# Two heads of attention share the products with their inverse sums; the norm of x is spread over the context's FFN, and that FFN's last products move to its end

## The chip, the cores and the metric

The kernel runs on one core of a Trainium2 chip. The metric is device time in microseconds (us), the median of several runs. One further execution is recorded by the hardware profiler; the profile gives its own time and its span, from its first instruction to its last.

## The reference, cut to what matters

Two layers work on a stream x of 512 tokens and a context of 256 tokens, both 1024 wide and in float32. A layer normalises its input, projects it, mixes it (attention, a Fourier mixer, a long convolution), projects the mix back and adds it; then it normalises again and applies a gated feed-forward network (FFN) with a convolution over three neighbouring tokens. The context is updated in the first layer only.

```python
s = einsum('bqhgd,bkhd->bhgqk', q, k) * (HEAD_DIM ** -0.5)   # 8 heads of 64, 2 kv heads
p = softmax(s, axis=-1)                                      # x sees 768 keys, the context 256
attn = einsum('bhgqk,bkhd->bqhgd', p, v)
...
u = dwconv3(h @ w_up, w_c, b_c)                              # 1024 -> 2 * 2816
gate, val = split(u, 2)
y = (silu(gate) * val) @ w_down                              # 2816 -> 1024
...
ctx = ctx + cga2 * rmsnorm(yc, g_post_ffn[i])                # first layer only
hc  = rmsnorm(ctx, g_pre_mix[1]) * (1.0 + csc1) + csh1       # what the second layer reads of it
```

## The kernel before, in words

**Products.** TensorE multiplies in a short float format, so each float32 factor is split into a high and a low part (`split`: a cast on ScalarE, L179, and a subtraction on VectorE or GpSimd, L180), and three products (`mm3`, L194 to L196) make one. Weights are loaded by SyncE's DMA queue into two buffers `Wr` (or `L`, `Wm`), and split into `Wh` and `Wl`.

**Order.** The kernel is written with Python generators. `go` runs a main piece and lets fillers run between its steps; `add` queues a filler in a lane; `need` runs a filler to its end. A table `Z` of waits and shares decides when each may go on. The tile framework then places the instructions of each engine in a fixed order; an engine takes its instructions in that order only.

**Attention** (`scores`, `attention`, `attention_small`, `head_out`). For a head and a tile of 128 queries, TensorE makes the scores, VectorE their maximum (L1010), ScalarE the exponentials `p` and their sum `den` (L1014). TensorE turns `p` (L1059), the halves of the turned tile `pT` are made, and TensorE multiplies them with the values (L1046) into `acc`, which holds the head's output as channels by queries, 64 rows from the high values and 64 from the low ones. To divide by the sums, TensorE multiplies the inverse sums, broadcast along 128 columns, with the identity (L1051 for x, four products a head; L1120 for the context, two a head): every row of the result `rb` holds the inverse sum of each query. `head_out` adds the two halves of `acc` (L1130, L1131) and multiplies them with `rb` (L1132), on 64 of the 128 partitions, because two heads share one tile `mix`. The scores run about one head ahead of the products with the values.

**First layer, second half.** `mix_out` of x leaves four tiles of x and queues, for each, the norm that the FFN of x reads (`norm_tile7`: four products with a diagonal matrix `dg`, L361, and four scalings on VectorE, L435, for each half tile; for tiles 2 and 3 also sums of tiles, L446 to L451, and splits `h<-xr` on VectorE and GpSimd). These norms, named `norm_xf0` to `norm_xf3`, are fillers of the context's FFN (`ffn_c`). That FFN makes 22 blocks m of 128 channels (`up`: 48 products, then the convolution L655 to L657, silu, the gate multiply on GpSimd L1301, and the split into `gc`), and after each second block the down products of the two blocks before (`ffn_down`, added to `y` at L1249). The last two blocks' down products are kept as a generator `rest_c`. Then `norm_xf3` must be done, and the FFN of x (`ffn_x`) runs: 22 blocks m, each with seven half-size products of sums of tiles and of weights. The sums of weights, `tt`, are made by GpSimd (L1348 to L1351, `prep`), then split (`Wh<-tt`, `Wl<-tt`). The entry `'RC': 3` puts `rest_c` behind block 3 of `ffn_x`. `rest_c` ends with the residual of the context (`rstd`, L221 to L227; L1155), and queues `tail_c`: the norm of the context for the second layer (`norm_tile`, with the scalings on VectorE, L404, or on ScalarE, L406, as its argument `dve` says; `NC` holds that argument), whose result is stored to memory.

Of the kernel before, what the change touches and what calls it, by code (L numbers as in the profile page):

```python
# [11 lines left out]
AF = mybir.ActivationFunctionType  # L12
ALU = mybir.AluOpType
# [4 lines left out]
P = 128  # L18
# [33 lines left out]
C512, C256, CTR, CF512 = 0.216, 0.109, 0.109, 0.86  # L52
# [13 lines left out]
class Net:  # L66
# [930 lines left out]
    def scores(self, st, h, t):  # L997
        nc = self.nc
        NK = 768 if st is self.X else 256
        kv = h // (NH // NKV)  # L1000
        hp = 1024 // st.T
        Q = st.Q[h // hp][:, h % hp]
        segs = [(0, 512), (512, 768)] if NK == 768 else [(0, 256)]
        ps = self.pw()
        qs = slice(t * P, (t + 1) * P)
        for a, b in segs:
            nc.tensor.matmul(ps[:, a:b], Q[:, qs], self.KD_[kv][:, a:b], start=True, stop=False)
            nc.tensor.matmul(ps[:, a:b], Q[:, qs], self.KL_[kv][:, a:b], start=False, stop=True)
        nm = self.small("nmax", 1, 4)
        nc.vector.tensor_reduce(nm, ps[:, :NK], axis=AX.X, op=ALU.max, negate=True)  # L1010
        p = self.M("p", F32)[:, :NK]
        if t == 0:
            st.den[h] = self.small("den", 4, 3)
        nc.scalar.activation(p, ps[:, :NK], AF.Exp, bias=nm, scale=1.0, accum_out=st.den[h][:, t : t + 1])  # L1014
        st.p[h, t] = p
        if t == st.NT - 1:
            nc.vector.reciprocal(st.den[h][:, : st.NT], st.den[h][:, : st.NT])
        return 2 * C512 * NK / 512

    def attention(self, st):  # L1020
        nc = self.nc
        NKT = 6 if st is self.X else 2
        T, NT = st.T, st.NT
        st.p, st.den = {}, {}
        todo = [(h, t) for h in range(NH) for t in range(NT)]
        lead = NT + Z["lead"]

        def ahead(n):
            c = 0.0
            for _ in range(n):  # L1030
                if todo:
                    c += self.scores(st, *todo.pop(0))
            return c

        yield ahead(2), Z["at0"]
        yield ahead(lead - 2), Z["at1"]
        LAG = 2
        acc, pts = {}, {}

        def pv(h, kt):  # L1040
            if kt == 0:
                acc[h] = self.pn()[:, :T]
            v = self.V_[h // (NH // NKV)][:, kt]
            pT = pts.pop((h, kt))
            for e in range(2):
                nc.tensor.matmul(acc[h], v, pT[:, e], start=kt == 0 and e == 0, stop=kt == NKT - 1 and e == 1)  # L1046
            if kt < NKT - 1:
                return 2 * C512 * T / 512
            rb = self.pn()[:, :T]
            for t in range(NT):  # L1050
                nc.tensor.matmul(rb[:, t * P : (t + 1) * P], st.den[h][:, t : t + 1].broadcast_to([P, P]), self.ident, start=True, stop=True)  # L1051
            self.head_out(st, h, acc[h], rb)
            return NT * 0.22 + 2 * C512 * T / 512

        steps = [(h, kt) for h in range(NH) for kt in range(NKT)]
        for i, (h, kt) in enumerate(steps):
            pt = self.pn()
            for t in range(NT):
                nc.tensor.transpose(pt[:, t * P : (t + 1) * P], st.p[h, t][:, kt * P : (kt + 1) * P], self.ident)  # L1059
            pT = self.M("pT").rearrange("p (e t) -> p e t", e=2)[:, :, :T]  # L1060
            self.split(pT[:, 0], pT[:, 1], pt[:, :T])
            pts[h, kt] = pT
            c = NT * CTR
            if NKT == 6:
                c += ahead(1 if kt < NT else 0)
            else:
                c += ahead(1)
            if i >= LAG:
                c += pv(*steps[i - LAG])
            yield c, 0.0  # L1070
        for i in range(LAG):
            yield pv(*steps[len(steps) - LAG + i]), 0.0

    def attention_small(self, st):

        nc = self.nc
        T, NT = st.T, st.NT
# [3 lines left out]
        for i in range(NH + 2):  # L1081
            c = 0.0
            if i < NH:
                kv = i // g
                Q = st.Q[i // hp][:, i % hp]
                ps = self.pn()
                sc = ps.rearrange("p (t k) -> p t k", t=NT)
                for t in range(NT):
                    qs = slice(t * P, (t + 1) * P)
                    nc.tensor.matmul(sc[:, t], Q[:, qs], self.KD_[kv][:, 0:T], start=True, stop=False)  # L1090
                    nc.tensor.matmul(sc[:, t], Q[:, qs], self.KL_[kv][:, 0:T], start=False, stop=True)
                nm = self.small("nmax2", NT, 4)
                nc.vector.tensor_reduce(nm, sc, axis=AX.X, op=ALU.max, negate=True)
                p = self.M("p", F32)[:, : NT * T].rearrange("p (t k) -> p t k", t=NT)
                den = self.small("den", 4, 3)
                for t in range(NT):
                    nc.scalar.activation(p[:, t], sc[:, t], AF.Exp, bias=nm[:, t : t + 1], scale=1.0, accum_out=den[:, t : t + 1])
                nc.vector.reciprocal(den[:, :NT], den[:, :NT])
                ps_[i], dens[i] = p, den
                c += 4 * C256  # L1100
            if 0 <= i - 1 < NH:
                p = ps_.pop(i - 1)
# [7 lines left out]
                c += 4 * CTR  # L1110
            if i >= 2:
                h = i - 2
                pT, den = pTs.pop(h), dens.pop(h)
                ps = self.pn()
                acc, rb = ps[:, 0:T], ps[:, T : 2 * T]
                for kt in range(NT):
                    for e in range(2):
                        nc.tensor.matmul(acc, self.V_[h // g][:, kt], pT[:, e, kt * T : (kt + 1) * T], start=kt == 0 and e == 0, stop=kt == NT - 1 and e == 1)
                for t in range(NT):
                    nc.tensor.matmul(rb[:, t * P : (t + 1) * P], den[:, t : t + 1].broadcast_to([P, P]), self.ident, start=True, stop=True)  # L1120
                self.head_out(st, h, acc, rb)
                c += 4 * C256 + NT * 0.22
            yield c, Z["as"]

    def head_out(self, st, h, acc, rb):
        nc = self.nc
        b0 = 64 * (h % 2)
        me, ot = slice(b0, b0 + 64), slice(64 - b0, 128 - b0)
        tf, of = self.T(st.T, "tf"), self.T(st.T, "of")
        nc.scalar.copy(tf[me], acc[ot])  # L1130
        nc.vector.tensor_tensor(of[me], acc[me], tf[me], op=ALU.add)  # L1131
        nc.vector.tensor_tensor(self.mixf(st, h // 2)[me], of[me], rb[me], op=ALU.mult)  # L1132
# [147 lines left out]
    def ffn_c(self, l):  # L1280
# [183 lines left out]
    def run(self):  # L1464
# [27 lines left out]
        for l in range(2):  # L1492
# [284 lines left out]
```

## Time and profile before

| what | value |
|---|---|
| median of 3 runs | 1768.56 us (1767.65 to 1769.28) |
| the profiled execution: its time | 1770.96 us |
| the profiled execution: its span | 1769.2 us |
| TensorE (PE) busy with products | 1640.4 us, 93% |
| VectorE (DVE) | 1391.0 us, 79% |
| ScalarE (ACT) | 949.8 us, 54% |
| GpSimd (POOL) | 672.2 us, 38% |
| mean granted clock of TensorE | 0.969 |

Every table of the profile is of the one profiled execution. A busy share over the whole span mixes stages; a stage is read with the windows view, which gives the busy time of each engine between two times and the granted clock (PEclk, 1.00 is full speed). The waits view says who waited for whom. A group row reads: line, engine, operation, output<-inputs, shapes, count | busy us, mean ns of one | idle us of the engine just before them.

### The profile page before, as it was taken

The numbers are of one execution on the slowest core, as the hardware profiler recorded it, in microseconds if no ns is written. First come the engines' busy times: TensorE is split into PE (matmuls) and PEld (weight loads), VectorE is DVE, ScalarE is ACT, GpSimd is POOL, SyncE is SP. The second block draws the span as 40 slices with busy tenths as digits, with TensorE's granted clock in tenths as the row PEclk, the third lists the DMA queues.
The fourth block names the chain that finished last, engine by engine and source line by source line (L and its number), as shares of the span: only waits on it lengthen the run. The fifth ranks groups of instructions, "written<-read, shape, count | busy, mean of one in ns | idle before, by whom it ended". The sixth has DMA issues, their size and how long they took to land. (4 is left out here: it accounts for less than half of the span.)

```text
span 1769.2 us, 27894 instructions
## 1 busy us (share of the span) xinstructions
PE 1640.4 (93%) x10534; PEld 1400.9 (79%) x10534; DVE 1391.0 (79%) x2269; ACT 949.8 (54%) x1787; POOL 672.2 (38%) x495
## 2 busy tenths in 40 slices
PE   6899988899999998998899998998899799999997
PEld 2677765787788897887889985787787678999995
DVE  3776667697666698888899997668895978989996
ACT  3554354586565454555555555534874455555553
POOL 2342212000134348664465545312002456555543
PEclk9899998999999998999999998999999799999999
DMA  9224377603476642233243358654012343323323
GB/s 361 92 77 140 88 226 267 231 11 143 164 254 229 227 153 82 86 108 96 72 138 113 96 168 320 214 176 132 1 48 82 128 137 119 105 88 106 96 74 129
DMA packets 75314, 246.69 MB, mean 139 GB/s; under 512 B 8111, under 2 KB 9647, under 8 KB 75180
## 3 DMA queue, kind: packets, MB, share of 16 engines
q1 hardware_dynamic: 66348, 215.54, 36.4%
q0 software_dynamic: 8832, 29.37, 5.4%
q8 instruction: 83, 1.36, 0.3%
q14 instruction: 51, 0.42, 0.1%
HBM read 230.72 MB, written 14.16 MB: 138 GB/s over the span
## 5 line engine op out<-in xcount | busy, mean ns | idle before, releaser
L194 PE MATMUL pn<-h,Wh 128*128 128x256 f32 x1328 | 374.4, 284 | 10.9 <-DVE C L1398 3.4
L196 PE MATMUL pn<-h,Wl 128*128 128x256 f32 x1328 | 370.2, 282 | 7.6 <-DVE Wl L180 7.6
L195 PE MATMUL pn<-h,Wh 128*128 128x256 f32 x1328 | 371.9, 281 | 1.9 <-POOL h L180 1.9
L194 PEld LDWEIGHTS pn<-h,Wh 128*128 128x128 f32 x1328 | 251.8, 190 | 21.2 <-issue 4.4
L196 PEld LDWEIGHTS pn<-h,Wl 128*128 128x128 f32 x1328 | 251.3, 190 | 11.7 <-DVE Wl L180 9.0
L195 PEld LDWEIGHTS pn<-h,Wh 128*128 128x128 f32 x1328 | 252.7, 190 | 5.9 <-POOL h L180 2.1
L179 ACT CAST Wh<-Wr 128x1024 fp32r<-128x1024 f32 x118 | 123.5, 1050 | 137.3 <-PE pn L195 63.1
L1348 POOL TENSOR_TENSOR tt<-r,r 128x512 f32<-128x512 f32 x44 | 66.0, 1501 | 260.7 <-DMA r<-w_up 224.8
L180 DVE TENSOR_TENSOR Wl<-Wr,Wh 128x1024 fp32r<-128x1024 f32 x89 | 121.5, 1367 | 53.2 <-ACT Wh L179 52.7
L195 PE MATMUL pw<-Wl,gT 128*128 128x512 f32 x352 | 141.0, 401 | 2.0 <-DVE Wl L180 2.0
L194 PE MATMUL pw<-Wh,gT 128*128 128x512 f32 x352 | 136.3, 403 | 5.3 <-ACT Wh L179 2.6
L196 PE MATMUL pw<-Wh,gT 128*128 128x512 f32 x352 | 139.7, 398 | 0.0
L180 DVE TENSOR_TENSOR Wl<-tt,Wh 128x1024 fp32r<-128x1024 f32 x88 | 129.8, 1495 | 7.5 <-ACT Wh L179 7.5
L1407 POOL TENSOR_TENSOR ft<-ft,ft 128x512 f32<-128x512 f32 x44 | 66.6, 1513 | 145.0 <-DVE ft L657 78.6
L179 ACT CAST Wh<-tt 128x1024 fp32r<-128x1024 f32 x88 | 91.1, 1047 | 51.5 <-PE pw L196 32.3
L180 POOL TENSOR_TENSOR h<-tf,h 128x256 fp32r<-128x256 f32 (+1 forms) x40 | 40.3, 1028 | 177.0 <-ACT h L179 177.0
L180 POOL TENSOR_TENSOR Wl<-Wr,Wh 128x1024 fp32r<-128x1024 f32 x29 | 72.8, 2516 | 61.3 <-ACT Wh L179 61.1
L1350 POOL TENSOR_TENSOR tt<-r,tt 128x512 f32<-128x512 f32 x44 | 83.9, 1907 | 13.5 <-DVE Wl L180 13.5
L655 ACT ACTIVATE ft<-C,vec 128x512 f32<-128x512 f32 x88 | 68.9, 811 | 34.3 <-DVE C L1395 20.0
L194 PE MATMUL pw<-h,Wh 128*128 128x256 f32 (+1 forms) x224 | 76.0, 339 | 9.8 <-DVE y L1249 2.7
L292 PE MATMUL pn<-wm,cpad 128*32 128x256 f32 x768 | 69.9, 433 | 15.2 <-DMA wm<-w_mod 14.9
L1278 DVE TENSOR_TENSOR y<-y,pw 128x1024 f32<-128x1024 f32 x64 | 77.3, 1212 | 7.8 <-PE pw L196 7.7
(379 smaller groups left out, 4696.6 us busy)
## 6 DMA issues: line engine op xcount, KB each, us to landing
wm<-w_mod SPq DMA_DIRECT2D x96, 512.0 KB, 5.0
r<-w_up SPq DMA_DIRECT2D x90, 512.0 KB, 3.6
Wr<-w_down SPq DMA_DIRECT2D x66, 512.0 KB, 3.9
L<-w_up SPq DMA_DIRECT2D x44, 512.0 KB, 4.3
Wr<-w_out SPq DMA_DIRECT2D x24, 512.0 KB, 3.6
Wr<-w_in_t SPq DMA_DIRECT2D x16, 512.0 KB, 3.9
dft<-hdft_x POOLq DMA_DIRECT2D x16, 512.0 KB, 4.1
Wr<-w_in_c SPq DMA_DIRECT2D x12, 512.0 KB, 3.6
```

Source lines behind the costliest of these rows:

```text
L179: r = nc.scalar.copy(hi, src)
L180: (el or nc.vector).tensor_tensor(lo, src, f32(hi), op=ALU.subtract)
L194: nc.tensor.matmul(ps, l[0], r[0], start=first, stop=False, **kw)
L195: nc.tensor.matmul(ps, l[0], r[1], start=False, stop=False, **kw)
L196: nc.tensor.matmul(ps, l[1], r[0], start=False, stop=last, **kw)
L292: nc.tensor.matmul(ps[32 * g : 32 * g + 32, cs], self.cpad[:, q % 2 * 4 + g, :], w[:, g, :], start=q % 2 == 0, stop=q % 2 == 1, skip_group ...
L655: nc.scalar.activation(dst, ps, AF.Identity, scale=w1, bias=b)
L1278: nc.vector.tensor_tensor(y, y, ps, op=ALU.add)
L1348: te.tensor_tensor(half(t13, 0), half(r[1], 0), half(r[0], 0), op=ALU.subtract)
L1350: te.tensor_tensor(half(t24, 0), half(r[1], 1), half(t13, 0), op=ALU.subtract)
L1407: nc.gpsimd.tensor_tensor(o[0], o[0], o[1], op=ALU.mult)
```

## The change

1. **Heads in pairs.** The sums of two heads go into one tile `den`. When the odd head's last sum is there, a new function `spread` takes the inverse and copies it into a tile `db`, 64 columns for the one head and 64 for the other (on GpSimd for x, on VectorE for the context). `head_out` of the even head only adds the halves of `acc`; that of the odd head makes the products of `db` with the identity for both heads, and multiplies all 128 partitions at once. `db` and the tile `of`, which now lives from the even head to the odd one, are of the ring of five buffers T.
2. **Norms of x spread.** `'XS': [1, 3, 5, 7]`: the groups 1, 3, 5 and 7 (of 11) of the context's FFN begin with `need("norm_xf0")` to `need("norm_xf3")`.
3. **The context's last products.** `'RC': -2`: `rest_c` runs right after `ffn_c`, ahead of `ffn_x`.
4. **The context's norm for the second layer.** `NC = None, 0`: all of its scalings go to ScalarE.

The diff, of the one-line table `Z` the changed entries alone:

```diff
+'XS': [1, 3, 5, 7]
-'RC': 3
+'RC': -2
...
-NC = None, 4
+NC = None, 0
...
-        if t == 0:
-            st.den[h] = self.small("den", 4, 3)
-        nc.scalar.activation(p, ps[:, :NK], AF.Exp, bias=nm, scale=1.0, accum_out=st.den[h][:, t : t + 1])
+        if t == 0 and h % 2 == 0:
+            st.den[h] = st.den[h + 1] = self.small("den", 8, 3).rearrange("p (t h) -> p t h", h=2)
+        nc.scalar.activation(p, ps[:, :NK], AF.Exp, bias=nm, scale=1.0, accum_out=st.den[h][:, t, h % 2 : h % 2 + 1])
         st.p[h, t] = p
-        if t == st.NT - 1:
-            nc.vector.reciprocal(st.den[h][:, : st.NT], st.den[h][:, : st.NT])
+        if t == st.NT - 1 and h % 2:
+            st.den[h] = self.spread(st, st.den[h])
...
-            rb = self.pn()[:, :T]
-            for t in range(NT):
-                nc.tensor.matmul(rb[:, t * P : (t + 1) * P], st.den[h][:, t : t + 1].broadcast_to([P, P]), self.ident, start=True, stop=True)
-            self.head_out(st, h, acc[h], rb)
+            self.head_out(st, h, acc[h], self.pn()[:, :T] if h % 2 else None, st.den[h])
...
+    def spread(self, st, den):
+
+        db = self.T(st.NT * P, "db")
+        self.nc.vector.reciprocal(den, den)
+        (self.nc.gpsimd if st is self.X else self.nc.vector).tensor_copy(db.rearrange("p (t h d) -> p t h d", h=2, d=64), den.unsqueeze(3).broadcast_to([P, st.NT, 2, 64]))
+        return db
...
-        tf, of = self.T(st.T, "tf"), self.T(st.T, "of")
+        tf = self.T(st.T, "tf")
+        if h % 2 == 0:
+            st.of = self.T(st.T, "of")
         nc.scalar.copy(tf[me], acc[ot])
-        nc.vector.tensor_tensor(of[me], acc[me], tf[me], op=ALU.add)
-        nc.vector.tensor_tensor(self.mixf(st, h // 2)[me], of[me], rb[me], op=ALU.mult)
+        nc.vector.tensor_tensor(st.of[me], acc[me], tf[me], op=ALU.add)
+        if h % 2:
+            for t in range(st.NT):
+                nc.tensor.matmul(rb[:, t * P : (t + 1) * P], den[:, t * P : (t + 1) * P], self.ident, start=True, stop=True)
+            nc.vector.tensor_tensor(self.mixf(st, h // 2), st.of, rb, op=ALU.mult)
...
         for i, ms in enumerate(groups):
+            if i in Z["XS"]:
+                self.need(f"norm_xf{Z['XS'].index(i)}")
...
                 self.go("ffn_c", self.ffn_c(l), Z["go_ffn_c"])
+                if Z["RC"] == -2:
+                    self.go("rest_c", self.rest_c, Z["go_ffn_c"])
                 self.need("norm_xf3")
```

`attention_small` is changed in the same way. How the orders move, at three places (the numbers behind the names are the buffers' own; the changed file's L1259, L1311, L1360 to L1363 and L1255 are L1249, L1301, L1348 to L1351 and L1245 of the kernel before):

VectorE in the context's FFN: L435 are the scalings of x's norm (tiles xr_4236, 4238, 4240 and 4242 before, xr_4192 to 4198 now), L1249 and L1259 the additions that end each group's down products. Before:

```order
L435 TENSOR_SCALAR xr_4236<-pn_4794,modA_2739,modB_2740 128x128 x4
...
L1249 TENSOR_TENSOR y_4808<-y_4808,pw_6329 128x1024
...
L435 TENSOR_SCALAR xr_4236<-pn_6412,modA_2739,modB_2740 128x128 x4
...
L435 TENSOR_SCALAR xr_4238<-pn_6498,modA_2739,modB_2740 128x128 x4
...
L435 TENSOR_SCALAR xr_4242<-pn_6839,modA_2739,modB_2740 128x128 x4
...
L1249 TENSOR_TENSOR y_4807<-y_4807,pw_6987 128x1024
```

And now:

```order
L435 TENSOR_SCALAR xr_4192<-pn_4932,modA_2731,modB_2732 128x128 x4
...
L1259 TENSOR_TENSOR y_4764<-y_4764,pw_5265 128x1024
...
L435 TENSOR_SCALAR xr_4194<-pn_5366,modA_2731,modB_2732 128x128 x4
...
L1259 TENSOR_TENSOR y_4764<-y_4764,pw_5722 128x1024
...
L435 TENSOR_SCALAR xr_4196<-pn_5809,modA_2731,modB_2732 128x128 x4
...
L1259 TENSOR_TENSOR y_4764<-y_4764,pw_6176 128x1024
...
L435 TENSOR_SCALAR xr_4198<-pn_6272,modA_2731,modB_2732 128x128 x4
```

Before, seven of the eight half tiles of the norm stood in the last groups of the context's FFN; now the tiles stand one or two groups apart, and none of them in the last groups.

GpSimd at the end of the context's FFN: ft_7015 (before) and ft_6971 (now) is the gate multiply of the last block; tt are the sums of weights for blocks 0 and 1 of the FFN of x. Before:

```order
L1348 TENSOR_TENSOR tt_7098<-r_7091,r_7090 128x512
L1349 TENSOR_TENSOR tt_7098<-r_7091 128x512
L1301 TENSOR_TENSOR ft_6901<-ft_6901 128x256
L1350 TENSOR_TENSOR tt_7099<-r_7091,tt_7098 128x512
L1348 TENSOR_TENSOR tt_7140<-r_7133,r_7132 128x512
L1349 TENSOR_TENSOR tt_7140<-r_7133 128x512
L180 TENSOR_TENSOR Wl_7137<-r_7132,Wh_7136 128x1024
L1351 TENSOR_TENSOR tt_7099<-tt_7099,r_7090 128x512
L1301 TENSOR_TENSOR ft_7015<-ft_7015 128x256
L1350 TENSOR_TENSOR tt_7141<-r_7133,tt_7140 128x512
```

And now:

```order
L1311 TENSOR_TENSOR ft_6971<-ft_6971 128x256
L180 TENSOR_TENSOR Wl_7153<-r_7148,Wh_7152 128x1024
L1360 TENSOR_TENSOR tt_7114<-r_7107,r_7106 128x512
L1361 TENSOR_TENSOR tt_7114<-r_7107 128x512
L1362 TENSOR_TENSOR tt_7115<-r_7107,tt_7114 128x512
L1360 TENSOR_TENSOR tt_7156<-r_7149,r_7148 128x512
L1361 TENSOR_TENSOR tt_7156<-r_7149 128x512
L1255 TENSOR_TENSOR y_4763<-y_4763,G_5466 128x512
L1363 TENSOR_TENSOR tt_7115<-tt_7115,r_7106 128x512
L1255 TENSOR_TENSOR y_4763<-y_4763,G_5466 128x512
L1255 TENSOR_TENSOR y_4764<-y_4764,G_5466 128x512 x2
L1362 TENSOR_TENSOR tt_7157<-r_7149,tt_7156 128x512
```

Six of the eight sums of weights stood ahead of the last gate multiply; now all eight stand behind it, with the context's own multiplications (L1255) among them.

TensorE at the same place: pn_7056 (before) and pn_7012 (now) are the last `up` products, pn_7197 and pn_7213 the first that read a split sum of weights. Before:

```order
L196 MATMUL pn_7056<-h_4440,Wl_7053 128x256
L194 MATMUL pn_7105<-h_6421,Wh_7094 128x256
...
L194 MATMUL pw_6987<-Wh_6983,gc_6725 128x512
...
L194 MATMUL pw_7088<-h_4803,Wh_7094 128x256
...
L194 MATMUL pn_7197<-h_6749,Wh_7176 128x256
...
L194 MATMUL pw_7747<-Wh_7731,gc_6970 128x512
```

And now:

```order
L196 MATMUL pn_7012<-h_4396,Wl_7009 128x256
L194 MATMUL pw_7062<-Wh_7046,gc_6926 128x512
...
L194 MATMUL pn_7121<-h_4941,Wh_7110 128x256
...
L194 MATMUL pw_7062<-Wh_7052,gc_6926 128x512
...
L194 MATMUL pw_7104<-h_4759,Wh_7110 128x256
...
L194 MATMUL pn_7213<-h_5840,Wh_7192 128x256
```

`rest_c` (pw_7747 before, pw_7062 now) stood some 380 rows behind pn_7197; it now starts right behind the last `up` product. Between that product and pn_7213 stand 24 products of `rest_c` and 48 of `ffn_x` that need no sum of weights.

More of the change, by code (lines that the diff above doesn't have):

```diff
@@ L57 @@
 RT = True
-Z = {'HV': [[[0], [1]], [[0, 1], []], [[], [0], [], [1]]], 'go_mod00': 1.0, 'go_norm_c': 0.3, 'go_hyp_c': 0.5, 'go_kvf_c': 0.5, 'go_q_c': 0.5, 'go_out_c': 1.0, 'go_ffn_c': 0.1, 'go_ffn': [0.1, 0.1], 'SH0': [0.7, 0.7, 0.7, 0.4, 0.5], 'SH1': [0.7, 0.7, 0.7, 0.5, 0.5], 'w_norm_x': 0.0, 'w_attn_c': 0.0, 'w_four_c': 2.0, 'w_norm_cf': 12.0, 'w_gate00': 0.0, 'w_mod_f0': 0.0, 'w_mod10': 8.0, 'w_gate10': 0.0, 'w_mod_f1': 0.0, 'w_taps': 0.0, 'mlat1': 1.0, 'mlat0': 1.2, 'mlat2': 2.0, 'lat': 7.0, 'nt': 0.8, 'nt7': 0.8, 'mg': 2.0, 'hy0': 1.0, 'hy1': 7.0, 'hy2': 14.0, 'tp0': 9.0, 'tp1': 2.5, 'tp2': 1.5, 'tp3': 2.0, 'at0': 1.5, 'at1': 2.0, 'as': 3.5, 'lead': 1, 'wx1': 9.0, 'QK0': [3.0, 7.0, 3.0, 6.0], 'QK1': [5.0, 7.0, 3.0, 6.0], 'TC': [50.0, 10.0, 10.0], 'BG': [0.15, 0.3], 'WN': [9.0, 7.0], 'ND': [3, 4], 'GF': ['Wm', 2.0, 0.0], 'MD': [4, 4, 4, 4], 'DG': [15, 15, 0], 'RC': 3, 'TW': 0.5, 'KE': 4, 'MT': 3, 'PO': [['k', 'f', 'v'], ['f', 'k', 'v']], 'EF': 1, 'E0': 4, 'lane_k': 4, 'el_na': 2, 'el_nx1': 4, 'ec': 3, 'CT': ['T', 'Q', 'T'], 'FX': 1, 'OC': 'qhHkayf'}
+Z = {'XS': [1, 3, 5, 7], 'HV': [[[0], [1]], [[0, 1], []], [[], [0], [], [1]]], 'go_mod00': 1.0, 'go_norm_c': 0.3, 'go_hyp_c': 0.5, 'go_kvf_c': 0.5, 'go_q_c': 0.5, 'go_out_c': 1.0, 'go_ffn_c': 0.1, 'go_ffn': [0.1, 0.1], 'SH0': [0.7, 0.7, 0.7, 0.4, 0.5], 'SH1': [0.7, 0.7, 0.7, 0.5, 0.5], 'w_norm_x': 0.0, 'w_attn_c': 0.0, 'w_four_c': 2.0, 'w_norm_cf': 12.0, 'w_gate00': 0.0, 'w_mod_f0': 0.0, 'w_mod10': 8.0, 'w_gate10': 0.0, 'w_mod_f1': 0.0, 'w_taps': 0.0, 'mlat1': 1.0, 'mlat0': 1.2, 'mlat2': 2.0, 'lat': 7.0, 'nt': 0.8, 'nt7': 0.8, 'mg': 2.0, 'hy0': 1.0, 'hy1': 7.0, 'hy2': 14.0, 'tp0': 9.0, 'tp1': 2.5, 'tp2': 1.5, 'tp3': 2.0, 'at0': 1.5, 'at1': 2.0, 'as': 3.5, 'lead': 1, 'wx1': 9.0, 'QK0': [3.0, 7.0, 3.0, 6.0], 'QK1': [5.0, 7.0, 3.0, 6.0], 'TC': [50.0, 10.0, 10.0], 'BG': [0.15, 0.3], 'WN': [9.0, 7.0], 'ND': [3, 4], 'GF': ['Wm', 2.0, 0.0], 'MD': [4, 4, 4, 4], 'DG': [15, 15, 0], 'RC': -2, 'TW': 0.5, 'KE': 4, 'MT': 3, 'PO': [['k', 'f', 'v'], ['f', 'k', 'v']], 'EF': 1, 'E0': 4, 'lane_k': 4, 'el_na': 2, 'el_nx1': 4, 'ec': 3, 'CT': ['T', 'Q', 'T'], 'FX': 1, 'OC': 'qhHkayf'}
 NF = 2, 4
 OR = "", "hcyqkf"
-NC = None, 4
+NC = None, 0
 CE = True
@@ L1048, in pv @@
                 return 2 * C512 * T / 512
-            rb = self.pn()[:, :T]
-            for t in range(NT):
-                nc.tensor.matmul(rb[:, t * P : (t + 1) * P], st.den[h][:, t : t + 1].broadcast_to([P, P]), self.ident, start=True, stop=True)
-            self.head_out(st, h, acc[h], rb)
-            return NT * 0.22 + 2 * C512 * T / 512
+            self.head_out(st, h, acc[h], self.pn()[:, :T] if h % 2 else None, st.den[h])
+            return h % 2 * NT * 0.22 + 2 * C512 * T / 512
         steps = [(h, kt) for h in range(NH) for kt in range(NKT)]
@@ L1094, in attention_small @@
                 p = self.M("p", F32)[:, : NT * T].rearrange("p (t k) -> p t k", t=NT)
-                den = self.small("den", 4, 3)
+                if i % 2 == 0:
+                    den = self.small("den", 8, 3)[:, : 2 * NT].rearrange("p (t h) -> p t h", h=2)
                 for t in range(NT):
-                    nc.scalar.activation(p[:, t], sc[:, t], AF.Exp, bias=nm[:, t : t + 1], scale=1.0, accum_out=den[:, t : t + 1])
-                nc.vector.reciprocal(den[:, :NT], den[:, :NT])
-                ps_[i], dens[i] = p, den
+                    nc.scalar.activation(p[:, t], sc[:, t], AF.Exp, bias=nm[:, t : t + 1], scale=1.0, accum_out=den[:, t, i % 2 : i % 2 + 1])
+                if i % 2:
+                    den = dens[i] = self.spread(st, den)
+                ps_[i] = p
                 c += 4 * C256
@@ L1112, in attention_small @@
                 h = i - 2
-                pT, den = pTs.pop(h), dens.pop(h)
+                pT, dn = pTs.pop(h), dens.pop(h, None)
                 ps = self.pn()
@@ L1118, in attention_small, with head_out @@
                         nc.tensor.matmul(acc, self.V_[h // g][:, kt], pT[:, e, kt * T : (kt + 1) * T], start=kt == 0 and e == 0, stop=kt == NT - 1 and e == 1)
[L1119 to L1122, printed above, removed]
+                self.head_out(st, h, acc, rb if h % 2 else None, dn)
+                c += 4 * C256 + h % 2 * NT * 0.22
             yield c, Z["as"]
-    def head_out(self, st, h, acc, rb):
+    def spread(self, st, den):
[3 more added lines that the diff above has]
+        return db
+    def head_out(self, st, h, acc, rb, den):
         nc = self.nc
```

## Prediction

> **What bounds the kernel now.** I read the page first, then windows over the stages that the change touches, then the waits of TensorE there.
>
> ```profile
> span 1769.2 us, 27894 instructions
> ...
> PE 1640.4 (93%) x10534; PEld 1400.9 (79%) x10534; DVE 1391.0 (79%) x2269; ACT 949.8 (54%) x1787; POOL 672.2 (38%) x495
> ...
> 550.00:650.00 100.00, 100.00 (x714) 88.37 (x714) 70.21 (x106) 51.46 (x78) 44.21 (x27) 1.00 0.62 207
> 650.00:725.00 75.00, 65.58 (x477) 62.06 (x476) 67.41 (x80) 35.69 (x61) 53.73 (x31) 0.93 0.27 81
> 725.00:825.00 100.00, 88.97 (x550) 79.84 (x549) 85.43 (x94) 56.54 (x90) 53.98 (x32) 0.93 0.36 111
> 825.00:925.00 100.00, 91.49 (x626) 84.64 (x624) 88.75 (x124) 57.25 (x90) 54.93 (x34) 0.97 0.31 101
> ...
> 1425.00:1525.00 100.00, 92.28 (x654) 82.87 (x654) 89.36 (x94) 56.27 (x88) 59.99 (x38) 1.00 0.36 120
> 1525.00:1625.00 100.00, 100.00 (x694) 92.47 (x693) 92.25 (x105) 52.11 (x83) 52.45 (x31) 1.00 0.34 106
> ```
>
> A window row holds the window, its length, then the busy time of PE, PEld, DVE, ACT, POOL, then PEclk. TensorE bounds most of the program: in 550 to 650, the context's FFN, it is busy for all of 100 us, with VectorE at 70. The end of that FFN and the first 200 us of x's FFN are different. What is lost there is at most the idle time plus the clock's loss over the window: 650 to 725 loses 9.4 + 0.07 x 75 = 14.7 us, 725 to 825 loses 11.0 + 7.0 = 18.0, and 825 to 925 loses 8.5 + 3.0 = 11.5; together 44.2. The second layer's FFN of x, the same loop with no context in it, loses 7.7 us in its first 100 us shown (1425 to 1525) and nothing in the next. So what the context does inside that loop is dear. The waits of TensorE in 650 to 930 (us in total, times, longest):
>
> ```profile
> PE pn L361 <- DVE dg L348: 5.6, 2, 4.4
> PE pn L196 <- DVE Wl L180: 5.2, 3, 4.0
> PE pn L194 <- ACT C L1391: 4.0, 2, 2.2
> PE pn L194 <- DVE C L1398: 3.4, 2, 3.1
> ...
> PE pw L195 <- DVE Wl L180: 2.0, 1, 2.0
> ```
>
> VectorE is late nearly everywhere: at 4.0 us (a split of the context's weights, while the norms of x pile up), and at `dg` of the context's norm.
>
> **The products with the inverse sums.** One head of x in attention, and the window of that head:
>
> ```profile
> 371.10:380.20 9.10, 9.10 (x62) 8.08 (x61) 8.93 (x15) 7.78 (x16) 0.00 (x0) 1.00 0.00 0
> ...
> 380.83 1.05 PE L1051 MATMUL pn<-ident,den 128*128 128x128 f32 x8
> 381.72 0.60 PE L1059 MATMUL pn<-ident,p 128*128 128x128 f32 x4
> ...
> L1132 DVE TENSOR_TENSOR mix<-of,pn 64x512 f32<-64x512 f32 x2 | 1.4, 686 | 0.1
> ...
> 250.00:300.00 50.00, 40.67 (x322) 30.82 (x321) 34.27 (x75) 23.97 (x75) 12.34 (x14) 0.93 0.72 242
> ```
>
> The four products (eight records) hold TensorE from 380.83 to the next product at 381.72, 0.89 us. A stationary `db` of 128 columns is as large as the broadcast it replaces, so I price it alike. Half of 16 heads' go: 8 x 0.89 = 7.1 us. TensorE is busy for 9.10 of 9.10 us, so all of it is on the path, if VectorE can follow: it is busy for 8.93, so 17.86 per pair. It loses one L1132 (0.69) per pair, which leaves 17.17 against TensorE's 18.20 - 0.89 = 17.31. VectorE is next, and only just behind; I take 7.1 and keep 5 as the lower end.
>
> For the context a head has two products, 0.45 us at the same pitch; four heads' go, 1.8 us. There (250 to 300) TensorE is busy for 40.67 of 50 us only, so I take 0.9, between 0 and 1.8. VectorE loses four multiplications and gains four copies of about their size: nothing.
>
> The eight copies of x go to GpSimd, idle (0.00) in attention; in the rows of this size below it takes 1.5 to 1.9 us, and the sums of a pair are there about a head (9.1 us) ahead of its products: covered. What the copies might do is hold VectorE:
>
> ```profile
> 666.22 2.49 DVE L180 TENSOR_TENSOR h<-s,h 128x512 fp32r<-128x512 f32 x1
> ...
> 702.94 0.41 DVE L1372 TENSOR_TENSOR C<-C,pn 128x256 f32<-128x256 f32 x1
> ...
> L1372 DVE TENSOR_TENSOR C<-C,pn 128x256 f32<-128x256 f32 x44 | 18.0, 409 | 3.9 <-ACT C L1370 2.4 <-PE pn L196 1.2 <-ACT h L179 0.3
> ```
>
> With GpSimd busy beside both, the first, whose inputs are both tiles of SBUF, takes 2.49 us for 512 columns, while the second, with one input in PSUM (pn), takes 0.41, its mean over 44. In attention every large instruction of VectorE reads pn or pw, so I add nothing; held by all eight copies it would be 15.2 us. The Trainium skill speaks against copies on GpSimd beside a busy VectorE (SBUF — State Buffer, Who interferes with whom): GpSimd and a VectorE instruction with two SBUF inputs exclude one another for the whole instruction, and one with at most one SBUF input is free. The trace agrees in both halves; by this the sum stays.
>
> **The norms of x.** They do the same work earlier, in 480 to 640, where VectorE has 30 us of 100 free (550 to 650): cost nothing. What they leave is the burst: the 4.0 us wait and most of the 14.7 us of 650 to 725 go.
>
> **The new end of the context's FFN.** TensorE now needs the last gate for `rest_c`, and GpSimd's queue has eight sums of weights behind that gate's multiplication.
>
> ```profile
> L1348 POOL TENSOR_TENSOR tt<-r,r 128x512 f32<-128x512 f32 x44 | 66.0, 1501 | 260.7 <-DMA r<-w_up 224.8 <-DVE ft L657 16.7 <-DVE Wl L180 8.2
> L1349 POOL TENSOR_TENSOR tt<-r 128x512 f32<-128x512 f32 x44 | 76.0, 1728 | 0.0
> L1350 POOL TENSOR_TENSOR tt<-r,tt 128x512 f32<-128x512 f32 x44 | 83.9, 1907 | 13.5 <-DVE Wl L180 13.5
> L1351 POOL TENSOR_TENSOR tt<-tt,r 128x512 f32<-128x512 f32 x44 | 73.0, 1660 | 2.9
> L180 POOL TENSOR_TENSOR Wl<-Wr,Wh 128x1024 fp32r<-128x1024 f32 x29 | 72.8, 2516 | 61.3 <-ACT Wh L179 61.1
> L1245 POOL TENSOR_TENSOR y<-y,G 128x512 f32<-128x512 f32 x20 | 26.3, 1328 | 27.2 <-ACT junk L231 27.2
> L1301 POOL TENSOR_TENSOR ft<-ft 128x256 f32<-128x256 f32 x22 | 18.8, 854 | 44.4 <-DVE ft L657 43.4 <-ACT ft L655 1.1
> ...
> L179 ACT CAST Wh<-tt 128x1024 fp32r<-128x1024 f32 x88 | 91.1, 1047 | 51.5 <-PE pw L196 32.3 <-POOL tt L1351 15.7 <-PE pn L195 3.5
> L655 ACT ACTIVATE ft<-pn,vec 128x256 f32<-128x256 f32 x44 | 24.5, 558 | 0.0
> L657 DVE SCALAR_TENSOR_TENSOR ft<-pn,vec,ft 128x255 f32<-128x255 f32 x44 | 21.0, 478 | 0.8
> L179 ACT CAST gc<-ft 128x256 fp32r<-128x256 f32 x22 | 8.9, 403 | 17.5 <-POOL ft L1301 17.4
> ...
> 601.61 0.40 PE L196 MATMUL pw<-Wh,gc 128*128 128x512 f32 x1
> 601.85 0.28 PE L194 MATMUL pn<-h,Wh 128*128 128x256 f32 x1
> 601.96 0.28 PE L195 MATMUL pn<-h,Wh 128*128 128x256 f32 x1
> ```
>
> Count from the end of the last `up` product. The gate takes L655 0.56, two L657 0.96, L1301 0.85 and the cast 0.40, together 2.8. TensorE passes a wide product in 0.24 (601.61 to 601.85) and a narrow one in 0.11; the order gives it six wide and four narrow ones meanwhile, 1.9. It waits for 0.9, with the hand-overs 1.3. GpSimd ends the gate at 2.4; then stand a split 2.5, L1348 1.5, L1349 1.7, L1350 1.9, L1348 1.5, L1349 1.7, L1245 1.3 and L1351 1.7, so block 0's sums are ready at 16.2 and cast at 17.3. TensorE has 24 x 0.24 + 48 x 0.11 = 11.0 us of products until then, so with the first wait it stands at 12.3 and waits 5.0. Block 1's sums are ready 3 x 1.3 + 1.9 + 1.7 = 7.5 later, at 23.7, and cast at 24.7. TensorE, going on at 17.3, passes 48 narrow products (5.3) and stands at 22.6: 2.1 more, if GpSimd goes on without a break. A wait of 5 us has a price in clock:
>
> ```profile
> 675.40:682.20 6.80, 3.36 (x15) 3.36 (x16) 6.80 (x8) 2.13 (x4) 6.80 (x5) 0.50 0.22 77
> 777.80:781.20 3.40, 3.40 (x9) 2.63 (x9) 3.07 (x4) 1.07 (x2) 3.40 (x4) 0.50 0.47 154
> 846.00:852.80 6.80, 6.13 (x28) 6.13 (x29) 5.94 (x9) 0.37 (x2) 1.85 (x1) 0.50 0.25 77
> ```
>
> After the 4.0 us and the 4.4 us wait the clock is half for 6.8 us, at most 3.4 lost; after the 2.0 us wait, for 3.4 us. So this place costs 1.3 + 5.0 + 2.1 + 3.4 = 11.8 us. All of it stands on one queue; between 6 (the sums' inputs early) and 20 (each sum half as long again, and both halves late) I take 11.8.
>
> **What stays in x's FFN.** `rest_c`'s 24 products are only moved. Its four additions, its squares, and the split of its weights leave the loop, and with them waits of the kinds C and Wl above. I take the loop's first 100 us as the second layer's, 7.7 lost, between 5 and 18 (as now). The residual and the norm of the context still come inside: `dg` 5.6 plus the clock's 3.4 (846 to 852.8), 9.0, between 3 and 12.
>
> ```profile
> L404 DVE TENSOR_SCALAR tf<-pn,modA,modB 128x128 f32<-128x128 f32 x80 | 27.7, 401 | 6.9 <-PE pn L359 3.9 <-PE pn L361 2.3 <-POOL h L180 0.7
> ...
> L406 ACT ACTIVATE tf<-pn,modB,modA 128x128 f32<-128x128 f32 x32 | 13.0, 471 | 8.6 <-DVE tf L404 6.4 <-DVE rs_t L213 2.3
> ```
>
> Sixteen scalings leave VectorE (16 x 0.40 = 6.4 us) for ScalarE (16 x 0.47 = 7.5), which is at 57 of 100 us there: nothing by itself, and VectorE's relief is in the 7.7.
>
> **The sum.** Lost after the change: 11.8 + 7.7 + 9.0 = 28.5, where 44.2 were lost: 15.7 gained. With attention's 7.1 and 0.9 it is 23.7. The profiled execution took 1770.96 us (1.8 more than its span): 1747.3. The median of the runs, 1768.56, lies 2.4 below that execution, so I predict 1744.9.
>
> By the Trainium skill (TensorE: Matmul & The Clock Gate, What's actually happening) the clock falls only after an idle window of about 3.4 us. The wait of 2.0 us ahead of 777.8 contradicts it here; by the rule the 7.0 of clock in 725 to 825 would not be won, and the time would be 1751.9.
>
> **The rivals.** About 0.2% (3.5 us) is what a measurement of this kernel can tell from no change.
> - *The queue eats the move* (0.16): the end of the context's FFN costs 20 us and x's FFN still loses 18 + 6. Then 44 are lost as now, and attention's 8.0 alone is left: 1760.6. For it: 14 instructions behind one gate; against: the second layer's loop runs with the same GpSimd work at 60 of 100 us.
> - *The context leaves no trace in x's FFN* (0.12): the first place costs 6, the loop 5, `dg` 3: 14 lost, 30 gained, 1730.4. For it: VectorE's relief; against: the chain to `dg` is the same one.
> - *VectorE bounds attention* (0.05): the copies hold it after all, 1.9 a pair. Then a pair takes 17.17 + 1.9 = 19.1 for 18.2 now, eight times 0.9 lost instead of 7.1 won: 1759.
> - *Slower* (0.06): GpSimd, ScalarE's cast and VectorE's split make a chain in which each waits for the other (as 2.49 for a split shows), TensorE runs it at half clock, and x's FFN begins without any lead. The place costs 25, the next 200 us lose 18 each as 725 to 825 does: 61 for 44.2, less 8.0: 9 us slower, 1777. It decides if block 1's sums land over 35 us after the last `up` product, where I have 25.
>
> **How the numbers follow.** My forecast (1736 to 1754 by itself) has 0.61. The range 1729 to 1762 takes in the first three rivals. Faster by over 0.2% is below 1765.0: all but the last case and a bit of the first, 0.90; within it 0.04; slower 0.06.
>
> **What would show it.** Right: x's heads in attention at a pitch of 8.65 us per head instead of 9.1, TensorE still full; no wait for a split of the context's weights before the FFN's end; one wait of about 5 us of TensorE for `Wh<-tt`, released by ScalarE behind GpSimd; PE at over 92 of 100 us in the first 100 us of x's FFN. Wrong: VectorE idle less than TensorE in attention; waits of over 10 us at the FFN's end; or `dg` waits of more than 6 us.

## The result, and the profile after

The changed kernel takes 1757.67 us (median of 11 runs, 1745.17 to 1767.67), the kernel before 1770.66 us in the same runs (1767.10 to 1778.38). The ratio is 0.9923, with a 95% interval of 0.9905 to 0.9941: by the ratio 13.6 us faster (10.4 to 16.8), where 23.7 was forecast. The time lies in the range of the prediction (1729 to 1762), but above the 1736 to 1754 of the forecast by itself. Measured again with the later experiments, the ratio was 0.9911 (0.9886 to 0.9936). The profiled execution took 1762.31 us, 4.6 more than the median.

**Heads of attention.** Two heads of x in the first and in the second layer, windows view, cut at the first score of one head and at that of the second head after it; first the kernel before (columns as in the prediction):

```profile
374.69:392.98 18.29, 18.29 (x122) 16.19 (x120) 17.20 (x26) 15.11 (x30) 0.00 (x0) 1.00 0.00 1
1274.94:1293.16 18.22, 18.22 (x121) 16.18 (x120) 17.56 (x27) 15.21 (x30) 0.00 (x0) 1.00 0.01 1
```

The same two heads after the change:

```profile
372.70:390.10 17.40, 17.40 (x113) 15.21 (x112) 16.59 (x25) 15.24 (x30) 0.61 (x1) 1.00 0.00 1
1264.16:1281.56 17.40, 17.40 (x113) 15.22 (x112) 16.59 (x25) 15.24 (x30) 0.62 (x1) 1.00 0.00 1
```

A pair takes 17.40 us where it took 18.29 and 18.22. TensorE is full in both; VectorE is at 16.59, and the copy on GpSimd takes 0.61.

**The context's FFN and x's FFN**, the windows of the prediction:

```profile
493.00:650.00 157.00, 154.87 (x1111) 135.49 (x1110) 115.94 (x172) 84.70 (x129) 71.00 (x45) 1.00 0.63 204
650.00:725.00 75.00, 65.66 (x448) 60.17 (x447) 56.00 (x65) 37.57 (x63) 47.63 (x30) 0.95 0.34 108
725.00:825.00 100.00, 91.94 (x631) 85.19 (x629) 84.45 (x111) 68.10 (x117) 52.35 (x35) 0.97 0.32 101
825.00:925.00 100.00, 98.10 (x678) 90.69 (x679) 92.41 (x105) 52.75 (x83) 51.90 (x32) 1.00 0.36 112
```

Idle time and clock together are 2.1 + (9.3 + 3.8) + (8.1 + 3.0) + 1.9 = 28.2 us. The prediction had 28.5 there, in place of 44.2. These windows lie at the same times in both kernels, not at the same work; the stages below follow the work.

What TensorE waits for there, 600 to 930 (us in total, times, longest):

```profile
PE pn L194 <- ACT Wh L179: 4.5, 4, 2.2
PE pn L361 <- DVE dg L348: 3.8, 1, 3.8
PE pn L196 <- DVE Wl L180: 3.5, 3, 1.7
PE pw L194 <- ACT gT L179: 2.2, 1, 2.2
PE pw L194 <- DVE y L1253: 2.1, 1, 2.1
```

The wait of 4.0 us for a split and one of the two waits for `dg` are gone. The end of the context's FFN has no single long wait: 2.2, 2.1, 1.6 and 1.7 us, 7.6 together, stand in the place of the 1.3, 5.0 and 2.1 of the prediction. Only one of the four is a wait that the prediction had (1.6, for the first block's sums of weights); the others are for a cast of x's weights that itself waited for a load (2.2), for an addition on VectorE, L1253 (2.1), and for a split of the first sums on VectorE (1.7).

**Where it did not go as forecast.** The end of x's FFN and the start of the second layer, 1030 to 1230, after:

```profile
PE pn L359 <- ACT y L378: 5.7, 2, 3.5
PE pn L292 <- DMA wm<-w_mod: 4.3, 1, 4.3
PE pw L194 <- ACT M L179: 1.7, 1, 1.7
```

The same place before, 1040 to 1240:

```profile
PE pw L195 <- DVE M L180: 2.9, 1, 2.9
PE pw L194 <- ACT M L179: 1.6, 1, 1.6
...
PE pn L292 <- DMA wm<-w_mod: 1.4, 1, 1.4
```

And ScalarE's queue ahead of the first exponentials of x's attention (start, us; L1014 makes `p`, and `Wh<-Wr` is a cast of weights for x's `w_out`), before:

```profile
335.49 2.23 ACT L179 CAST Wh<-Wr 128x1024 fp32r<-128x1024 f32 x2
...
342.91 1.04 ACT L179 CAST Wh<-Wr 128x1024 fp32r<-128x1024 f32 x1 [1.15 <-DMA Wr<-w_out]
343.97 1.28 ACT L1014 ACT_TABLE_LOAD   x1
345.26 0.90 ACT L1014 ACTIVATE p<-pw,nmax 128x768 f32<-128x768 f32 x1
...
347.03 1.04 ACT L179 CAST Wh<-Wr 128x1024 fp32r<-128x1024 f32 x1
```

After:

```profile
333.68 1.98 ACT L179 CAST Wh<-Wr 128x1024 fp32r<-128x1024 f32 x2
...
339.67 1.04 ACT L179 CAST Wh<-Wr 128x1024 fp32r<-128x1024 f32 x1 [1.27 <-DMA Wr<-w_out]
342.92 1.04 ACT L179 CAST Wh<-Wr 128x1024 fp32r<-128x1024 f32 x1 [2.21 <-DMA Wr<-w_out]
343.98 1.28 ACT L1014 ACT_TABLE_LOAD   x1
345.28 0.90 ACT L1014 ACTIVATE p<-pw,nmax 128x768 f32<-128x768 f32 x1
```

The fourth cast, which waits for its load, has moved ahead of the exponentials. TensorE, which came earlier than before, waits for them for 7.3 us in place of 5.2.

**By stages.** The program, cut at marks that both kernels have: the first score of the context's attention, of x's, the first product that reads `gc`, the 101st product of x's first FFN that reads `Wl` and `gT`, the first and the last score of x's attention in the second layer. us, one profiled execution each; both kernels were profiled twice.

| stage | before | after | pairs alone | move alone | products late again | norms not spread | cast held back | and weights late |
|---|---|---|---|---|---|---|---|---|
| to the context's attention | 238.7, 232.5 | 235.0, 233.7 | 231.6 | 232.5 | 238.6 | 232.8 | 235.0 | 234.3 |
| to x's first score | 68.7, 68.8 | 69.1, 69.1 | 67.9 | 69.4 | 68.7 | 68.8 | 68.7 | 69.2 |
| to the first `gc` | 190.4, 191.1 | 189.0, 189.2 | 188.0 | 190.9 | 188.9 | 187.8 | 186.3 | 186.7 |
| to the 101st `Wl,gT` | 463.3, 463.8 | 450.1, 448.8 | 460.4 | 449.6 | 453.9 | 456.6 | 448.6 | 450.1 |
| to layer 2's first score | 277.8, 279.5 | 285.9, 280.3 | 277.9 | 284.1 | 281.1 | 283.2 | 284.9 | 282.5 |
| to its last score | 70.9, 70.2 | 68.4, 68.4 | 68.3 | 70.9 | 68.0 | 68.4 | 68.0 | 66.1 |
| to the end | 459.3, 462.1 | 462.8, 458.0 | 461.0 | 463.9 | 461.5 | 462.4 | 462.9 | 462.3 |

From the means of two: the FFNs give 14.1, the two attentions of x 1.6 and 2.1, the last stage 0.3; the way to layer 2's attention takes back 4.4, that to x's first score 0.3. Together 13.4, as measured; the first stage, whose instructions are the same, is left out. The 4.4 is small against the spread of two executions of one kernel (285.9 and 280.3), but other kernels bear it out: this stage takes 277.8 to 279.5 us in the three profiles in which neither the norms nor the products are moved, and 280.3 to 285.9 in the ten in which at least one of them is.

### The profile page after: what moved, and what is told of

The parts are those of the page before. It is cut to its first block, busy times and chain, and to the rows that moved or that the text cites. A ratio compares the mean times of both kernels' runs of the same rounds, so it can differ in the third digit from the quotient of the medians.

```text
span 1760.2 us, 27774 instructions
## 1 busy us (share of the span) xinstructions
PE 1628.5 (93%) x10454; PEld 1386.5 (79%) x10454; DVE 1373.6 (78%) x2233; ACT 948.8 (54%) x1799; POOL 673.7 (38%) x503
## 5 line engine op out<-in xcount | busy, mean ns | idle before, releaser
L196 PEld LDWEIGHTS pn<-h,Wl 128*128 128x128 f32 x1328 | 249.7, 189 | 11.8 <-DVE Wl L180 8.5
L1360 POOL TENSOR_TENSOR tt<-r,r 128x512 f32<-128x512 f32 x44 | 65.6, 1490 | 184.1 <-DMA r<-w_up 151.0
L194 PEld LDWEIGHTS pw<-Wh,gT 128*128 128x128 f32 x352 | 64.4, 190 | 24.6 <-DVE y L1253 3.7
```

Of the source, the lines that this page charges most:

```text
L194: nc.tensor.matmul(ps, l[0], r[0], start=first, stop=False, **kw)
L196: nc.tensor.matmul(ps, l[1], r[0], start=False, stop=last, **kw)
L1360: te.tensor_tensor(half(t13, 0), half(r[1], 0), half(r[0], 0), op=ALU.subtract)
```

## The experiments

Theory A: the parts pay where the prediction says, and two new waits take some of it back (a cast ahead of the exponentials, and the start of the second layer). The rivals stand in each expectation.

**pairs_only.** The changed kernel with the three other entries as before.

```diff
-'XS': [1, 3, 5, 7] ... 'RC': -2 ... NC = None, 0
+'XS': [] ... 'RC': 3 ... NC = None, 4
```

> The heads in pairs alone; the norms of x, the context's last products and the context's scalings as before. Theory A (the parts add up, each at its place): x's heads run at 8.64 us each in both layers, as in the trace after, and that is worth 5 to 6 us of the time; the waits of TensorE at the end of the context's FFN and in x's FFN stay as before. Rival B (what is won ahead of a stage that waits for its weights is waited out there): the start of x's attention in layer 1 stands at 346 us after the span's start as in both traces, whatever TensorE won ahead of it, and the time is within 3 us of before.

Ratio to before 0.9960 (0.9942 to 0.9978): 7.1 us (3.9 to 10.3). The pairs gain 2.8 and 2.2 us in the two attentions, the context's perhaps 0.9. TensorE's wait for the exponentials ended at 341.6 us, not at 346: rival B falls, nothing is pinned to a time. That wait was 7.1 us here and 5.0 in move_only: it is the pairs that move the fourth cast ahead of the exponentials, not the other parts.

**move_only.** The kernel before with the norms spread, the products moved and the scalings on ScalarE.

```diff
+'XS': [1, 3, 5, 7] ... 'RC': -2 ... NC = None, 0
```

> The norms of x spread, the context's last products at its FFN's end and its scalings on ScalarE; the heads one by one as before. Theory A: from the first down product of the context to the last of x's FFN the time is 7 to 9 us shorter than before, and the whole as much: of 42 us of lost time before that FFN's 925 us mark about 27 are left, and up to 7 come back as a wait for the modulation's weights at the end of x's FFN. Rival B (that wait was chance of one execution): no wait over 2 us for these weights there, and 13 to 16 us faster than before. Rival C (GpSimd's queue eats the move): within 3 us of before.

Ratio 0.9927 (0.9907 to 0.9948): 12.9 us (9.2 to 16.5), more than the 7 to 9 of theory A, whose size was off. The FFNs take 14 less, as in the changed kernel, and the wait for the modulation's weights is there again (4.6 us): B and C fall. Pairs and move alone make 20.0 together, the change 13.6: 6.4 apart, where the three intervals (3.2, 3.6 and 3.2 to each side) allow 5.8 together. Whether the parts take something from each other stays open.

**after_rc3** and **after_noxs.** The changed kernel with one of the two moves undone.

```diff
-'RC': -2
+'RC': 3
```

> The changed kernel with the context's last products behind block 3 of x's FFN again. Theory A (the loop suffers from the context's work in it, as the prediction has it): 725 to 925 loses 20 us or more of idle time and clock again, where the changed kernel loses 13, while the 12 us of the context's FFN's end mostly go; 3 to 8 us slower than the changed kernel. Rival B (the spread norms alone carry the gain, the place of the last products is of no matter): within 2 us of the changed kernel.

```diff
-'XS': [1, 3, 5, 7]
+'XS': []
```

> The changed kernel without the spread: the norms of x pile up at the end of the context's FFN as before. Theory A: TensorE waits there for a split on VectorE (4 us before) and for the sums of weights as well; 8 to 15 us slower than the changed kernel. Rival B (the products moved to the FFN's end give the norms the time they need): within 3 us of the changed kernel.

Ratios 0.9943 (0.9923 to 0.9963) and 0.9948 (0.9929 to 0.9967): against the changed kernel's 0.9923 some 3.5 and 4.4 us slower, neither clear of noise (about 4.8 us for such a difference), but the stages say where. With the products back in the loop, windows view:

```profile
650.00:725.00 75.00, 69.25 (x533) 66.05 (x532) 60.57 (x71) 39.01 (x64) 49.14 (x30) 1.00 0.36 109
725.00:825.00 100.00, 86.46 (x548) 76.96 (x547) 78.96 (x86) 52.81 (x83) 54.19 (x34) 0.97 0.32 99
825.00:925.00 100.00, 94.60 (x638) 87.40 (x637) 87.77 (x115) 65.83 (x112) 48.16 (x33) 0.97 0.37 116
```

650 to 725 loses 5.8 us, 725 to 925 loses 18.9 of idle time and 6.0 of clock, where the changed kernel loses 13.1 and 13.0 in all. Without the spread the long wait is back (waits, 600 to 930):

```profile
PE pn L196 <- DVE Wl L180: 6.8, 3, 4.0
PE pn L361 <- DVE dg L348: 3.7, 1, 3.7
PE pw L194 <- DVE y L1259: 2.6, 1, 2.6
```

Each move without the other gains in the FFNs (463.5 to 453.9 for the norms, to 456.6 for the products), both together 14. A holds for the products; for the norms it was too large, 7.2 us in the stage and 4.4 in the whole where 8 to 15 were expected.

**cast_late.** One element of the fourth weights' tile is written first from the maximum of a late query tile, so that load and cast come after it.

```diff
+        if st is self.X and h == 0 and t == 3:
+            self.mk = self.small("mk", 1, 1)
+            nc.vector.tensor_copy(self.mk, nm)
...
+        if mark is not None:
+            self.nc.vector.tensor_copy(r[:, 0, 0:1], mark)
```

> The changed kernel with one cast of ScalarE's queue held back: the load of the fourth weights for x's mix takes a tile that is first written from the maximum of x's last query tile of head 0, so that this cast can't stand ahead of the first exponentials. Theory A (this cast, which waits for its load, is why TensorE waits 7.1 to 7.3 us for the first exponentials where the kernel before waits 5.0 to 5.2): the wait falls to 4 to 5.2 us and the time by 2 to 4 us against the changed kernel (1 to 2 ahead of that stage may be waited out again behind it). Rival B (the exponentials wait for something else, such as the residual of the context on VectorE): the wait stays at 7 us, and so does the time.

Ratio 0.9894 (0.9869 to 0.9919). TensorE's wait there (300 to 360), first after, then with the cast held back (its lines stand two lower in the file):

```profile
PE pw L1007 <- ACT p L1014: 7.8, 2, 7.3
```

```profile
PE pw L1009 <- ACT p L1016: 4.5, 3, 3.9
```

The wait falls to 3.9 us and the stage from 189.1 to 186.3: shown. The third cast waits for its load as before (1.1 us, 1.3 in the changed kernel), so it is the place of the fourth that counts. 2.8 us is what the cast costs; the whole time is 5.1 below the changed kernel's, which is not clear of noise by itself and has room for 2.8.

**half_fetch.** Half as many bytes for one read at the end of x's FFN: the kernel leaves out half of the context's normalised tile, and GpSimd writes zeros there (four writes of 0.55 us, which the other kernels do not have).

```diff
-                self.nc.gpsimd.dma_start(t, self.dr["h"][e, i])
+                self.nc.gpsimd.dma_start(t[:, :512], self.dr["h"][e, i][:, :512])
+                self.nc.gpsimd.memset(f32(t)[:, 512:], 0.0)
```

> The changed kernel with half of the context's normalised tile left out when it is read back at the end of x's first FFN: 1 MB less is loaded, and GpSimd fills that half with zeros. Theory A (the loads there, at 400 GB/s, are the bound, and TensorE's wait of 4.3 us for the modulation's weights is theirs): the wait falls below 2 us, the half clock behind it goes, and the time falls by 3 to 8 us. Rival B (the wait comes from the place of these loads in SyncE's queue, which is the same here): a wait of 3 us or more stays, and the time is within 2 us of the changed kernel.

Ratio 0.9907 (0.9887 to 0.9927), 2.8 us below the changed kernel's, not clear of noise. Waits, 1030 to 1230:

```profile
PE pw L195 <- DVE M L180: 5.5, 1, 5.5
PE pn L359 <- ACT y L378: 3.2, 1, 3.2
PE pn L292 <- DMA wm<-w_mod: 2.5, 2, 1.3
```

The longest wait for the weights falls to 1.3, as theory A has it. That it was one for bandwidth is not shown by this: the same wait is 4.3 and 2.6 us in two executions of the changed kernel, 2.5 in dve_copy, and 1.4 and 2.9 before. What is clear is that a split of the second layer's weights is now 5.5 us late, and the stage stays at 284.6. Both theories had left out what comes next.

**late_weights.** cast_late with slower pacing of the second layer's modulation.

```diff
-'mlat2': 2.0
+'mlat2': 6.0
```

> The changed kernel with the held-back cast of cast_late, and the products of the second layer's modulation paced at 6 us in place of 2 us each: between the modulation's products at the start of the last down products of x's FFN and the layer's end no product stands any more that needs a weight of the saturated stretch. Theory A (that wait for loads is what gives the gain of the move back): TensorE's wait of 3.75 us for these weights in cast_late is gone and with it the half clock, and the time falls by 3 to 6 us against cast_late. Rival B (what comes next, the splits of the first weights of the second layer, is as late): a wait of VectorE or ScalarE of 3 us or more takes its place, and the time is within 2 us of cast_late.

Ratio 0.9887 (0.9866 to 0.9909), as cast_late within the noise: rival B. Waits, 1030 to 1230:

```profile
PE pw L197 <- DVE M L180: 3.7, 1, 3.7
PE pn L361 <- ACT y L380: 3.1, 2, 1.9
PE pn L294 <- DMA wm<-w_mod: 2.7, 2, 2.0
```

The split of M is late again, in the place of the weights. Both stages to layer 2's last score take 348.6, where cast_late takes 352.9 and before 349.2; the two executions of the changed kernel take 354.3 and 348.7, so this difference is within their spread. This and cast_late are the shortest versions here, 1.1% below before, though not clear of noise against the changed kernel (0.9911 in the runs of late_weights).

**after_nc4** and **dve_copy.** The scalings as before; the copies of `db` on VectorE.

```diff
-NC = None, 0
+NC = None, 4
```

> The changed kernel with the context's scalings as before: four on VectorE, none on ScalarE, of each half tile. Theory A (VectorE's relief is worth little): within 3 us of the changed kernel, from 3 faster to 3 slower. Rival B (the scalings on ScalarE delay the queue that feeds x's FFN): 4 us or more faster. Rival C (VectorE's relief carries the gain of the loop): 4 us or more slower.

```diff
-        (self.nc.gpsimd if st is self.X else self.nc.vector).tensor_copy(
+        self.nc.vector.tensor_copy(
```

> The changed kernel with the eight copies of x's inverse sums on VectorE in place of GpSimd. Theory A (TensorE bounds attention and VectorE is only just behind, 17.17 of 17.31 us for a pair): a copy of 0.5 us puts VectorE ahead, a head takes 8.8 us where it takes 8.64, and the time is 1 to 4 us longer. Rival B (VectorE has more room than its busy time says): 8.64 stays, and the time is within 1.5 us.

Ratios 0.9919 (0.9897 to 0.9942) and 0.9930 (0.9909 to 0.9952). The scalings matter to neither side (theory A). The copies on VectorE, a pair of heads and the copies themselves (ns: least, median, most):

```profile
371.84:389.25 17.41, 17.41 (x113) 15.25 (x112) 16.75 (x27) 15.26 (x31) 0.00 (x0) 1.00 0.00 1
```

```profile
L1126 DVE COPY db<-den x12: 281/416/428, 251.2 to 1295.9; 128x512 f32<-128x512 f32 x8, 128x256 f32<-128x256 f32 x4
```

A pair takes 17.41 us on either engine: rival B. VectorE has 0.66 us of room in a pair even with the copy.

**after_again** and **before_again.** Both kernels unchanged, for second profiles.

> The changed kernel once more, unchanged, for a second profile of it on another execution. What belongs to the order of the instructions comes again: 7.1 to 7.3 us of wait ahead of the exponentials, heads at 8.6 to 8.7 us, 448 to 452 us from the first down product of the context to the hundredth product of x's FFN with a low half of weights, 3 us or more of wait for the modulation's weights. What was chance differs: the first 235 us, and the last 330 us, by up to 5 us each. The time: 12 to 15 us below before.

> The kernel before once more, unchanged, for a second profile. What belongs to the order comes again: a wait of 5.0 to 5.2 us ahead of the exponentials, 463 us to the hundredth product with a low half of weights (less 3 if a stretch of half clock is missing), 125 us from there to the end of x's FFN. What was chance differs: the first 239 and the last 325 us, by up to 7 us.

After again: 15.8 us below before (12 to 15 was expected), 7.1 us ahead of the exponentials, 17.41 us a pair, 448.8 us to the 101st product, and 2.6 us of wait for the weights (3 or more was expected). Before again: 5.1 us, 463.8, and 2.9 us of that last wait. So this wait alone does not separate the kernels, and the stage around it does so for these two by its means only (278.7 and 283.1, spread by 1.7 and 5.6). One wait there does: that for `y` on ScalarE ahead of the transposes of x's norm is 3.1 to 5.7 us in all nine profiles with the products moved, and at most 0.6 in the four without.

## Why the prediction was right and wrong

- **x's attention, 7.1: right for the heads, wrong for the stage.** A pair gains 0.89 and 0.82 us, where 0.89 was forecast. The stages gain 1.6 and 2.1, the first with eight more records of the products of x's norm (0.11 each) in it, the second with three of its four pairs. The failed step is that only GpSimd's and VectorE's queues were looked at: on ScalarE a cast moved ahead of the first exponentials, 2.8 us. With it held back the stages gain 4.4 and 2.5.
- **VectorE bounds attention (a rival): wrong**, shown by dve_copy. The estimate had VectorE at 17.17 of 17.31; it is at 16.59 of 17.40.
- **The context's attention, 0.9: nothing** in the changed kernel (68.75 to 69.1); the lower end of its bounds.
- **The norms and the end of the context's FFN: right in sum, in part by luck.** 13.1 us are lost in 650 to 725 (11.8 forecast for that end), but as four waits of about 2 us. The first sums of weights were ready 17.0 us after the last `up` product (16.2 forecast), but TensorE came to them at 17.4 and not at 12.3, mainly because two waits that the prediction did not have (2.2 and 2.1) stood ahead; so it waited 1.6 and not 5.0. One wait of 1.7 us for a split of the context's weights is left, at 618 us. After 2.2 us at 737.5 the clock is half, as after the 2.0 us wait of the prediction; so the Trainium skill's rule (TensorE: Matmul & The Clock Gate, What's actually happening), which asks for an idle window of about 3.4 us, disagrees with this trace again:

```profile
740.20:743.60 3.40, 3.40 (x14) 3.09 (x13) 3.40 (x4) 2.79 (x5) 1.61 (x1) 0.50 0.32 95
```

- **What stays in x's FFN: right.** 13.0 us in 725 to 925 (16.7 forecast). One `dg` wait of 3.8 is left, with 3.4 us of half clock behind it: 5.5 (9.0 forecast), and 7.5 for the rest of the loop (7.7). "The queue eats the move" and "slower" are out, and the reason is shown by after_rc3 and after_noxs: each move takes its own waits away.
- **The sum: this step failed.** It carried the 15.7 us of the FFNs to the end. They came (14.1), but the next stage takes 4.4 more: the loads of that place run at 400 GB/s (as they did before), the transposes of x's norm now wait for ScalarE (5.7 us, 0.6 before), and where the loads are relieved the split of the next weights is late. Which of these is the first cause is not settled: half_fetch and late_weights each shorten the wait for the weights, and another takes its place.

## What to carry to other kernels

A gain inside a stage is only a gain if the next stage is ready earlier too: read the first loads and the first splits behind the place of a change before its gain is carried to the end. In a program with fixed queues, compare the order of every engine around the changed stage, also those that the change does not name: here one cast that waits for a load, moved ahead of an exponential, cost more than a third of what the pairs gained.

## What the runs showed of the hardware that was not expected

The first stage of the table has the same instructions in all kernels, yet took 231.6 to 239.1 us. Two executions of the kernel before, 20 to 28 us, the first of 238.7 us and the second of 232.5 us in this stage:

```profile
20.00:28.00 8.00, 7.29 (x36) 2.36 (x28) 2.41 (x6) 2.52 (x6) 0.00 (x0) 1.00 1.03 410
```

```profile
20.00:28.00 8.00, 6.24 (x64) 2.39 (x56) 3.76 (x9) 3.74 (x8) 1.32 (x3) 1.00 1.03 410
```

One passes 36 products where the other passes 64, and the view prints a granted clock of 1.00 for both. In the first, that 1.00 is not a measurement: the trace's rows of the clock begin at 37.1 us there and at 20.4 us in the second, and ahead of the first row the view prints 1.00. The products show the pace (start, us):

```profile
22.87 1.93 PE L292 MATMUL pn<-wm,cpad 128*32 128x256 f32 x16
```

```profile
21.59 1.07 PE L292 MATMUL pn<-wm,cpad 128*32 128x256 f32 x16
```

The same sixteen products take 1.8 times as long, about what half clock costs elsewhere in these traces (narrow products 0.21 us apart at 0.50 after 702 us, 0.12 at 1.00). So it was most likely half clock without a row. Over all thirteen profiles the first row of the clock and the stage go together: 231.6 to 234.3 us in the six where it stands at 20 to 21 us, 233.7 in the one at 32 us, 235.0 to 239.1 in the six at 36 to 37 us.

A broadcast copy on GpSimd took 0.61 us for 512 columns, where in the prediction's rows the additions of that size took 1.5 to 1.9.
